# Row steps of 32x32 inverses moved to GpSimd, with other margins in a hand-written list schedule

## The chip, the cores and the metric

One core of a Trainium2 chip. The metric is the device time of one execution in microseconds; lower is better.

## The reference

One layer of a hybrid trunk on x of 512 x 1024 in float32: a mixer of four branches (Mamba-2, a gated linear recurrence, retention, RWKV-7) on one combined input projection, gated, merged and projected, then a convolutional feed-forward block, with root-mean-square norms between. The change touches the RWKV-7 branch, which for each of 16 heads of 64 runs this over 512 steps:

```python
def step(state, inp):
    r_t, w_t, k_t, v_t, kk_t, b_t = inp
    sk = jnp.einsum('bhvk,bhk->bhv', state, kk_t)
    state = (state * w_t[:, :, None, :] - sk[..., None] * b_t[:, :, None, :]
             + v_t[..., None] * k_t[:, :, None, :])
    return state, jnp.einsum('bhvk,bhk->bhv', state, r_t)
```

The kernel does it in chunks of 64 steps, so that each chunk needs the inverse of a unit triangular 64x64 matrix, which is put together from inverses of 32x32 blocks.

## The kernel before, in words

**Weights.** A weight block of 128 x 1024 is loaded by SP into `raw` (4 buffers, L452). `split` (L446) casts it on ACT to a high part `whi` (L447, 3 buffers) and takes the low part `wlo` on DVE (L448, 3 buffers). A product is three matmuls for each of 8 slices (L466 to L468): 24 matmuls of 128 x 512 a block, into one of three PSUM buffers `acc`. These are the long work of PE; all four branches, the gates, the output projection and the feed-forward block (from L1289) are made of them.

**RWKV in pairs of heads.** Eight pairs j run one behind the other. `rwkv_a1(j)` makes the projections and decays. `rwkv_a2(j)` builds the scaled operands (L701 on GpSimd, L702 to L705 on DVE), the products of a chunk with itself (L719), and the block matrices `ab`. These go to DRAM (`nd`, L764) and come back as `nt` (L767), one 32x32 matrix of 32 to a partition, its columns dealt out over four groups of partitions. Then 31 row steps follow (L769 to L775): each multiplies a column of `nt` with a row of `xr` into `prod` and adds that to the later rows of `xr`; (31 - jj) rows of jj//4 + 1 columns in step jj. Both instructions are on DVE. `xr` and a transposed copy (L777) go to DRAM as `xd` and `xtd` (L781, L782) and come back as `x11`, which has the buffer of `xr` (L787, shown as xr in the profile), and `tt` (L790). `rwkv_b(j)` joins the blocks with 32x32 matmuls (L801, L811) and runs the chunks in turn: L824, L826, L828, L829, L830, L832, L835. L869 makes the output, L870 sends it to DRAM for the branch product. Most tiles of a pair have one buffer, so pair j+1 reaches L719 when pair j is through its chunks.

**What fills PE meanwhile.** Generators give the other three branches and, once these are through, the branch products with their gates (L1217 to L1249) to fill PE. The last branch product (L1286) needs the RWKV output.

**The planner.** At the end `_order` (L390) takes all instructions of the program, plays them through a model of the five queues (`_run`, L236), improves the priorities in `_RUNS` rounds, keeps the best plan and ties each engine's instructions into that order; on the chip each engine follows it and waits where an operand is late. Costs stand in `_cost` (L114): for a GpSimd operation

```python
return 250.0 + n * (0.9 if kind == "InstMemset" else 1.0 if kind == "InstTensorCopy" else 2.4), _HOP
```

with n elements per partition and 60 ns for the way to another engine. On PE a "short" product (one that doesn't go to `acc`) comes ahead of weight products, but only if its operands have been ready for `_MARGIN` ns (L309); 32-row matmuls are `small`, those that follow each other in one tile stay together, and a change to or from them is charged 500 ns. A DMA is charged 450 ns of its queue, its bytes on a common wire at 330 bytes a ns, and 1500 ns until it has landed (L337, L338). A DVE operation of several operands that starts while GpSimd is busy is charged up to 0.7 of its time more (L327).

Of the kernel before, what the change touches and what calls it, by code (L numbers as in the profile page):

```python
# [15 lines left out]
P = 128  # L16
# [29 lines left out]
for _key in ([("lora", 0), ("lora", 1)]  # L46
# [16 lines left out]

_TABLES = {"Exp": ("exp",), "Tanh": ("exp", "sigmoid", "gelu", "silu"), "Sigmoid": ("sigmoid",), "Sqrt": ("sqrt",),
           "Gelu_apprx_tanh": ("gelu",), "Silu": ("silu",)}
_MARGIN = 50.0
_RUNS = 12
_HOP = 60.0
_SWITCH = 500.0


def _base(name):
# [74 lines left out]
def _graph(nc):  # L147


    import types  # L150
    E = mybir.EngineType
    ins = list(nc.cur_bb.bb.instructions)
    N = len(ins)
    preds = [set() for _ in range(N)]
    news, tiles_of = [[] for _ in range(N)], [[] for _ in range(N)]
    hist, users, tag_of, pool_of, queue, bufs = {}, {}, {}, {}, {}, {}
    released, gate, psum = [], {}, set()
    real, last_new, opener, after = [], {}, {}, [set() for _ in range(N)]
    small = [isinstance(i, mybir.InstMatmult) and i.ins[0].bass_ap.shape[0] <= 32 for i in ins]
    for k, i in enumerate(ins):  # L160
        if "Boundary" in type(i).__name__:
            text = i.concise()
            pool = text.split("pool=")[1].split()[0]
            if "op=release" in text:
                released.append(pool)
            else:
                gate[pool] = list(released)
            continue
        real.append(k)
        for write, args in ((False, i.ins), (True, i.outs)):  # L170
            for a in args:
                ap = getattr(a, "bass_ap", None)
                if ap is None or not hasattr(ap.tensor, "slot_key"):
                    continue
                t = ap.tensor
                name = t.name
                p0, p1, m = _region(ap)
                bank = t.space == bass.MemoryType.PSUM
                if name not in hist:
                    tag = str(t.slot_key())  # L180
                    hist[name], tag_of[name], users[name] = [], tag, []
                    if tag in last_new and last_new[tag] != k:
                        after[k].add(last_new[tag])
                    last_new[tag] = k
                    queue.setdefault(tag, []).append(name)
                    bufs[tag] = t.tag_meta.bufs or 1
                    pool_of[name] = tag.rstrip("')").split("_")[-2]
                    if bank:
                        psum.add(pool_of[name])
                    news[k].append(name)  # L190
                lst = hist[name]
                if opener.setdefault(name, k) != k:
                    after[k].add(opener[name])
                for o, w, q0, q1, b in lst:
                    if (write or w or bank) and o != k and q0 < p1 and p0 < q1 and b & m:
                        preds[k].add(o)
                if write or bank:
                    lst[:] = [x for x in lst if x[0] == k or not (p0 <= x[2] and x[3] <= p1 and x[4] & ~m == 0)]
                lst.append((k, write, p0, p1, m))
                if name not in tiles_of[k]:  # L200
                    tiles_of[k].insert(0 if write else len(tiles_of[k]), name)
                    users[name].append(k)
    for k in real:
        after[k] -= preds[k]
        preds[k] |= after[k]

    lead, last = {}, None
    for k in real:
        if ins[k].engine == E.PE:
            if not small[k]:  # L210
                last = None
            elif last is not None and tiles_of[last][0] == tiles_of[k][0]:
                lead[k] = last = lead[last]
            else:
                lead[k] = last = k
    for k, l in lead.items():
        preds[l] |= {o for o in preds[k] if lead.get(o) != l}
        after[l] |= {o for o in after[k] if lead.get(o) != l}
        if k != l:
            preds[k].add(l)  # L220
            after[k].add(l)
    succ = [[] for _ in range(N)]
    for k in real:
        for o in preds[k]:
            succ[o].append(k)
    gates = {}
    for p, old in gate.items():
        gates[p] = [q for q in old if (q in psum) == (p in psum)]
    acc = [i.engine == E.PE and _base(i.outs[0].bass_ap.tensor.name) == "acc" for i in ins]
    cost = [None] * N  # L230
    for k in real:
        cost[k] = _cost(ins[k])
    return types.SimpleNamespace(**locals())


def _run(g, prio, margin):  # L236
# [8 lines left out]
    engines = [E.PE, E.DVE, E.Activation, E.Pool, E.SP]  # L245
    free = {e: 0.0 for e in engines}
    pend, ready, order = {e: [] for e in engines}, {e: [] for e in engines}, {e: [] for e in engines}
    held, table, wire, was = [], "", 0.0, False
    queue = {t: list(q) for t, q in g.queue.items()}
    room = {t: [(0.0, "")] * b for t, b in g.bufs.items()}  # L250
    n_users = {t: len(u) for t, u in g.users.items()}
# [5 lines left out]
    def offer(k):  # L257
# [6 lines left out]
        for n in g.news[k]:  # L264
# [4 lines left out]
                behind.setdefault(k, []).append(old)  # L269
            for q in g.gates.get(g.pool_of[n], ()):  # L270
                est[k] = max(est[k], pool_end.get(q, 0.0))
        heapq.heappush(pend[ins[k].engine], (est[k], k))
        return True

    def try_held():
# [16 lines left out]
    while len(seq) < len(real):  # L292
        best = None
        for e in engines:
            if ready[e]:
                t = free[e]
            elif pend[e]:
                t = max(free[e], pend[e][0][0])
            else:
                continue  # L300
            if best is None or t < best[0]:
                best = (t, e)
        t, e = best
        while pend[e] and pend[e][0][0] <= t:
            k = heapq.heappop(pend[e])[1]
            heapq.heappush(ready[e], (-1.0 if g.lead.get(k, k) != k else prio[k], k))
        early = []
        if e == E.PE:
            while ready[e] and not g.acc[ready[e][0][1]] and ready[e][0][0] >= 0 and est[ready[e][0][1]] + margin > t:  # L309
                early.append(heapq.heappop(ready[e]))  # L310
            if early and not ready[e]:
                heapq.heapify(early)
                ready[e], early = early, []
        k = heapq.heappop(ready[e])[1]
        for x in early:
            heapq.heappush(ready[e], x)
        i = ins[k]
        dur, tail = g.cost[k]
        if e == E.Activation and type(i).__name__ == "InstActivation":
            sets = _TABLES.get(str(i.func).split(".")[-1])  # L320
            if sets and table not in sets:
                table = sets[0]
                dur += 1283.0
        if e == E.PE and g.small[k] != was:
            was = g.small[k]
            dur += _SWITCH
        if e == E.DVE and free[E.Pool] > t and len(i.ins) > 1 and not g.tiles_of[k][-1].startswith(("ra", "rb", "acc")):  # L327
            dur *= 1.0 + 0.7 * min(1.0, (free[E.Pool] - t) / dur)
        order[e].append(k)
# [4 lines left out]
        if type(i).__name__ == "InstDMACopy":  # L334
            free[e] = t + (450.0 if e == E.SP else 100.0)
            dur_of[k] = free[e] - t
            wire = max(wire, t + 450.0) + 4.0 * i.outs[0].bass_ap.size() / 330.0  # L337
            done[k] = wire + 1500.0  # L338
        opened = bool(g.news[k])
        for s in g.succ[k]:  # L340
            left[s] -= 1
            est[s] = max(est[s], t if k in g.after[s] else t + dur if ins[s].engine == e and e != E.SP else done[k])
            if not left[s]:
                if g.news[s]:
                    held.append(s)
# [16 lines left out]
def _latest(g, r, chained):  # L362
# [11 lines left out]
            for u in g.users[m]:  # L374
                need.setdefault(u, []).append(k)
    for k in reversed(r.seq):
        e = g.ins[k].engine
        whole = r.done[k] - r.start[k]
        v = r.end - whole
        if k in nxt:  # L380
            v = min(v, late[nxt[k]] - r.dur[k])
        for s in g.succ[k]:
            v = min(v, late[s] - (0.0 if k in g.after[s] else r.dur[k] if g.ins[s].engine == e and e != E.SP else whole))
        for s in need.get(k, ()):
            v = min(v, late[s] - whole)
        late[k] = v
# [3 lines left out]
def _order(tc, nc):  # L390
# [7 lines left out]
    for n in range(_RUNS):  # L398
# [1 line left out]
        if best is None or r.end < best.end:  # L400
            best = r
        late = _latest(g, r, [PE])
        prio = [first[k] if g.ins[k].engine == PE else late[k] for k in range(g.N)]
    behind = mybir.DependencyInfo(mybir.DependencyClass.NoSync, mybir.DependencyReason.DATA)
    for seq in best.order.values():
        for a, b in zip(seq, seq[1:]):
# [4 lines left out]
def tile_hybrid_block(ctx, tc, x, wts, wzdt, lora, lruw, cpack, consts, rettab, nfin, out):  # L411
# [37 lines left out]

    def wraw(kind, j):  # L450
        n = 1088 if kind == "zdt" else 1024
        raw = wp.tile([P, 1088], F32, name="raw", bufs=4)  # L452
        nc.sync.dma_start(out=raw[:, 0:n], in_=wzdt[j] if kind == "zdt" else wts[_BLK[(kind, j)]])
        return raw, n

    def wsplit(raw, n):
        hi = wp.tile([P, 1088], F32R, name="whi", bufs=3)
        lo = wp.tile([P, 1088], F32R, name="wlo", bufs=3)
        split(hi[:, 0:n], lo[:, 0:n], raw[:, 0:n])
        return hi, lo  # L460
# [232 lines left out]
    def rwkv_a2(j, prep):  # L693
# [76 lines left out]
        for jj in range(31):  # L770
            n, m = 31 - jj, jj // 4 + 1
            pr = rkb.tile([P, 32, 8], F32, name="prod", bufs=1)
            nc.vector.tensor_tensor(out=pr[:, 0:n, 0:m], in0=nt[:, jj, jj + 1:32].unsqueeze(2).broadcast_to([P, n, m]),
                                    in1=xr[:, jj:jj + 1, 0:m].broadcast_to([P, n, m]), op=ALU.mult)
            nc.vector.tensor_tensor(out=xr[:, jj + 1:32, 0:m], in0=xr[:, jj + 1:32, 0:m], in1=pr[:, 0:n, 0:m], op=ALU.add)  # L775
        xt = rkb.tile([P, 8, 32], F32, name="prod", bufs=1)
        nc.vector.tensor_copy(out=xt, in_=xr.rearrange("p i c -> p c i"))  # L777
        xd = dr.tile([16, 32, 32], F32, name="xd", bufs=2)
# [750 lines left out]
```

## Time and profile before

| what | value |
|---|---|
| median of 3 runs | 1600.75 us (1598.83 to 1601.36) |
| the profiled execution, device time | 1597.41 us |
| its span, first to last instruction | 1595.6 us |
| mean granted clock of TensorE | 0.981 |

PE is the matrix engine, PEld its weight loads, DVE the vector engine, ACT the scalar engine, POOL is GpSimd, SP the queue that issues nearly all DMAs. A name such as `raw<-in_wts_dram` tells the tile written and what is read. Each wait is put down to what ended it.

### The profile page before, as it was taken

The numbers are of one execution on the slowest core, as the hardware profiler recorded it, in microseconds if no ns is written. First come the engines' busy times: TensorE is split into PE (matmuls) and PEld (weight loads), VectorE is DVE, ScalarE is ACT, GpSimd is POOL, SyncE is SP. The second block draws the span as 40 slices with busy tenths as digits, with TensorE's granted clock in tenths as the row PEclk, the third lists the DMA queues.
The fourth block names the chain that finished last, engine by engine and source line by source line (L and its number), as shares of the span: only waits on it lengthen the run. The fifth ranks groups of instructions, "written<-read, shape, count | busy, mean of one in ns | idle before, by whom it ended". The sixth has DMA issues, their size and how long they took to land.

```text
span 1595.6 us, 22214 instructions
## 1 busy us (share of the span) xinstructions
PE 1546.5 (97%) x8324; PEld 1297.7 (81%) x8324; DVE 1085.2 (68%) x2334; ACT 733.9 (46%) x1198; POOL 60.7 (4%) x78
## 2 busy tenths in 40 slices
PE   7999989999999999999999999999999999999998
PEld 6878868887788888977878878888888888888886
DVE  6797888887888897887765966435335666566233
ACT  6653476447754585358422622323224544444123
POOL 0100000000001000001000100000000000000000
PEclk9999999999999998998999999999999999999999
DMA  5243233233143233353442432434232322323321
GB/s 207 81 126 85 79 109 106 80 106 97 54 144 105 69 104 101 97 163 112 153 128 67 148 102 74 149 103 132 95 130 95 106 92 95 104 92 109 102 94 53
DMA packets 108461, 169.46 MB, mean 106 GB/s; under 512 B 54833, under 2 KB 64305, under 8 KB 108353
## 3 DMA queue, kind: packets, MB, share of 16 engines
q1 hardware_dynamic: 107632, 166.92, 33.0%
q8 instruction: 66, 1.08, 0.3%
q10 hardware_dynamic: 720, 1.11, 0.2%
q14 instruction: 43, 0.34, 0.1%
HBM read 150.66 MB, written 15.24 MB: 104 GB/s over the span
## 4 chain that ended last, share of the span: by engine, by line
PE 85%; DVE 7%; DMA 3%; SPq 2%; ACT 1%; issue 1%; DVEq 0%; ACTq 0%
PE acc L467 19%; PE acc L466 19%; PE acc L468 19%; PE acc L1302 3%; PE acc L1303 3%; PE acc L1301 3%; PE rb L824 2%; PE acc L587 1%; PE ra L719 1%; PE acc L588 1%; PE acc L589 1%; PE rb L828 1%; SPq L782 1%; DVE wlo L448 1%; PE inn L443 1%
## 5 line engine op out<-in xcount | busy, mean ns | idle before, releaser
L466 PE MATMUL acc<-hh,whi 128*128 128x512 f32 (+1 forms) x1240 | 496.7, 401 | 6.3 <-DVE pr L611 4.3
L467 PE MATMUL acc<-hh,wlo 128*128 128x512 f32 (+1 forms) x1240 | 495.7, 400 | 0.5 <-DVE wlo L448 0.4
L468 PE MATMUL acc<-hl,whi 128*128 128x512 f32 (+1 forms) x1240 | 493.4, 398 | 0.1
L448 DVE TENSOR_TENSOR wlo<-raw,whi 128x1024 fp32r<-128x1024 f32 x228 | 278.7, 1224 | 206.5 <-ACT whi L447 205.4
L447 ACT CAST whi<-raw 128x1024 fp32r<-128x1024 f32 x228 | 239.1, 1049 | 390.0 <-PE acc L468 210.0
L466 PEld LDWEIGHTS acc<-hh,whi 128*128 128x128 f32 x1240 | 236.5, 191 | 51.3 <-DVE pr L611 5.2
L467 PEld LDWEIGHTS acc<-hh,wlo 128*128 128x128 f32 x1240 | 236.5, 191 | 43.7 <-issue 1.9
L468 PEld LDWEIGHTS acc<-hl,whi 128*128 128x128 f32 x1240 | 236.3, 191 | 42.6 <-issue 1.2
L468 PE MATMUL acc<-yl,whi 128*128 128x512 f32 x256 | 102.6, 401 | 0.0
L466 PE MATMUL acc<-yh,whi 128*128 128x512 f32 x256 | 102.5, 401 | 0.0
L467 PE MATMUL acc<-yh,wlo 128*128 128x512 f32 x256 | 102.2, 399 | 0.0
L587 PE MATMUL acc<-whi,hh 128*128 128x256 f32 (+1 forms) x256 | 78.1, 307 | 0.7 <-DVE sm L906 0.7
L588 PE MATMUL acc<-wlo,hh 128*128 128x256 f32 (+1 forms) x256 | 77.9, 305 | 0.0
L589 PE MATMUL acc<-whi,hl 128*128 128x256 f32 (+1 forms) x256 | 76.9, 301 | 0.0
L1301 PE MATMUL acc<-whi,gh 128*128 128x512 f32 x176 | 69.4, 395 | 0.0
L1303 PE MATMUL acc<-whi,gl 128*128 128x512 f32 x176 | 69.4, 395 | 0.0
L1302 PE MATMUL acc<-wlo,gh 128*128 128x512 f32 x176 | 69.4, 395 | 0.0
L1356 DVE SCALAR_TENSOR_TENSOR fc<-acc,fw,fc 128x511 f32<-128x511 f32 x88 | 65.7, 747 | 4.0 <-ACT fc L1354 2.5
L775 DVE TENSOR_TENSOR xr<-xr,prod 128x60 f32<-128x60 f32 (+24 forms) x248 | 56.9, 229 | 8.1
L468 PEld LDWEIGHTS acc<-yl,whi 128*128 128x128 f32 x256 | 48.6, 190 | 9.6 <-DVE yl L448 0.2
L466 PEld LDWEIGHTS acc<-yh,whi 128*128 128x128 f32 x256 | 48.6, 190 | 9.2
L906 DVE SCALAR_TENSOR_TENSOR sm<-acc,cp,sm 128x511 f32<-128x511 f32 (+2 forms) x72 | 53.6, 745 | 3.6 <-ACT sm L904 2.3
(334 smaller groups left out, 2454.8 us busy)
## 6 DMA issues: line engine op xcount, KB each, us to landing
raw<-in_wts_dram SPq DMA_DIRECT2D x226, 512.0 KB, 3.3
yr<-y SPq DMA_DIRECT2D x32, 256.0 KB, 3.5
y<-sm SPq DMA_DIRECT2D x24, 256.0 KB, 2.2
nt<-nd SPq DMA_DIRECT2D x32, 128.0 KB, 2.7
sm<-acd SPq DMA_DIRECT2D x16, 256.0 KB, 4.1
x<-in_x_dram SPq DMA_DIRECT2D x4, 512.0 KB, 6.2
sm<-sm SPq DMA_DIRECT2D x32, 64.0 KB, 2.0
ym<-bg SPq DMA_DIRECT2D x16, 128.0 KB, 1.8
```

What stands on the lines that cost most here:

```text
L447: nc.scalar.copy(out=hi, in_=src)
L448: nc.vector.tensor_tensor(out=lo, in0=src, in1=hi.bitcast(F32), op=ALU.subtract)
L466: nc.tensor.matmul(ps, wh, xh, start=first, stop=False)
L467: nc.tensor.matmul(ps, wl, xh, start=False, stop=False)
L468: nc.tensor.matmul(ps, wh, xl, start=False, stop=last)
L587: nc.tensor.matmul(o, hh[:, ko, t], wh[:, s], start=ko == 0, stop=False)
L588: nc.tensor.matmul(o, hh[:, ko, t], wl[:, s], start=False, stop=False)
L589: nc.tensor.matmul(o, hl[:, ko, t], wh[:, s], start=False, stop=ko == KT - 1)
L1301: nc.tensor.matmul(ps[i], xh[:, ko, t], w[0][:, s], start=ko == 0, stop=False)
L1302: nc.tensor.matmul(ps[i], xh[:, ko, t], w[1][:, s], start=False, stop=False)
L1303: nc.tensor.matmul(ps[i], xl[:, ko, t], w[0][:, s], start=False, stop=ko == 2 * nblk - 1)
L1356: nc.vector.scalar_tensor_tensor(out=t[:, s:], in0=ps[:, :S - s], scalar=fw[:, o + 2 - s:o + 3 - s], in1=t[:, s:], op0=ALU.mult, op1=ALU.add)
```

## The change

Both instructions of each of the 31 row steps go from DVE to GpSimd (62 for a pair of heads, 496 in all). `whi` has four buffers instead of three, `raw` three instead of four. In the planner: the margin of a short product is 100 ns instead of 50, and 300 ns where it is a 32-row matmul; a read into SBUF from the scratch tensors xd, xtd, y, ym or acd is charged 2500 ns instead of 1500 until it has landed; the first weight product after a short one is charged 17 ns more; eight rounds instead of twelve. Weight products and short ones have lists of their own (the choice between them follows the same rule as before).

```diff
-_MARGIN = 50.0
-_RUNS = 12
+_MARGIN = 100.0
+_RUNS = 8
 _HOP = 60.0
 _SWITCH = 500.0
+_BACK = 17.0
...
-        early = []
         if e == E.PE:
-            while ready[e] and not g.acc[ready[e][0][1]] and ready[e][0][0] >= 0 and est[ready[e][0][1]] + margin > t:
-                early.append(heapq.heappop(ready[e]))
-            if early and not ready[e]:
-                heapq.heapify(early)
-                ready[e], early = early, []
-        k = heapq.heappop(ready[e])[1]
-        for x in early:
-            heapq.heappush(ready[e], x)
+            while ready[e]:
+                k = heapq.heappop(ready[e])[1]
+                heapq.heappush(weights if g.acc[k] else shorts, (-1.0 if g.lead.get(k, k) != k else prio[k], k))
+            early = []
+            while shorts and shorts[0][0] >= 0 and est[shorts[0][1]] + (300.0 if g.small[shorts[0][1]] else margin) > t:
+                early.append(heapq.heappop(shorts))
+            if weights and not shorts:
+                k = heapq.heappop(weights)[1]
+            else:
+                if not shorts:
+                    shorts, early = early, []
+                    heapq.heapify(shorts)
+                k = heapq.heappop(shorts)[1]
+            for x in early:
+                heapq.heappush(shorts, x)
+        else:
+            k = heapq.heappop(ready[e])[1]
...
+            if not run and g.acc[k]:
+                dur += _BACK
+            run = run + 1 if g.acc[k] else 0
...
-            done[k] = wire + 1500.0
+            done[k] = wire + (2500.0 if i.outs[0].bass_ap.tensor.space != bass.MemoryType.DRAM and
+                              _base(i.ins[0].bass_ap.tensor.name) in ("xd", "xtd", "y", "ym", "acd") else 1500.0)
...
-        raw = wp.tile([P, 1088], F32, name="raw", bufs=4)
+        raw = wp.tile([P, 1088], F32, name="raw", bufs=3)
...
-        hi = wp.tile([P, 1088], F32R, name="whi", bufs=3)
+        hi = wp.tile([P, 1088], F32R, name="whi", bufs=4)
...
             pr = rkb.tile([P, 32, 8], F32, name="prod", bufs=1)
-            nc.vector.tensor_tensor(out=pr[:, 0:n, 0:m], in0=nt[:, jj, jj + 1:32].unsqueeze(2).broadcast_to([P, n, m]),
+            nc.gpsimd.tensor_tensor(out=pr[:, 0:n, 0:m], in0=nt[:, jj, jj + 1:32].unsqueeze(2).broadcast_to([P, n, m]),
                                     in1=xr[:, jj:jj + 1, 0:m].broadcast_to([P, n, m]), op=ALU.mult)
-            nc.vector.tensor_tensor(out=xr[:, jj + 1:32, 0:m], in0=xr[:, jj + 1:32, 0:m], in1=pr[:, 0:n, 0:m], op=ALU.add)
+            nc.gpsimd.tensor_tensor(out=xr[:, jj + 1:32, 0:m], in0=xr[:, jj + 1:32, 0:m], in1=pr[:, 0:n, 0:m], op=ALU.add)
```

## Rows read from the trace of the kernel before

**Rows 1.** The page: span, and busy time of each engine.

```profile
span 1595.6 us, 22214 instructions
...
PE 1546.5 (97%) x8324; PEld 1297.7 (81%) x8324; DVE 1085.2 (68%) x2334; ACT 733.9 (46%) x1198; POOL 60.7 (4%) x78
```

**Rows 2.** Busy time of each engine by stretch of 40 us, granted clock, DMA share.

```profile
120.00:160.00 40.00, 38.88 (x298) 35.28 (x298) 31.92 (x83) 13.05 (x25) 2.91 (x2) 0.91 0.33 85
480.00:520.00 40.00, 38.68 (x313) 35.40 (x312) 32.25 (x75) 16.44 (x42) 4.16 (x3) 0.96 0.37 105
600.00:640.00 40.00, 36.63 (x287) 33.54 (x286) 30.21 (x66) 23.16 (x46) 2.95 (x2) 0.87 0.32 88
720.00:760.00 40.00, 37.25 (x233) 30.55 (x232) 28.44 (x56) 31.59 (x48) 5.82 (x3) 0.83 0.40 119
800.00:840.00 40.00, 37.46 (x224) 30.49 (x222) 26.73 (x81) 12.21 (x20) 1.23 (x2) 0.97 0.42 119
840.00:880.00 40.00, 39.96 (x205) 33.59 (x205) 21.54 (x58) 9.64 (x19) 1.90 (x2) 0.95 0.22 71
1040.00:1080.00 40.00, 40.00 (x178) 33.11 (x177) 13.74 (x15) 9.34 (x11) 0.00 (x0) 1.00 0.27 93
```

**Rows 3.** PE's waits, longest in total first: total us, times, longest us.

```profile
PE inn L443 <- DVE nxn L504: 10.1, 1, 10.1
...
PE rb L801 <- DMA xr<-xd: 9.4, 10, 2.5
...
PE acc L466 <- DVE pr L611: 4.3, 1, 4.3
...
PE rb L811 <- DMA tt<-xtd: 3.1, 2, 2.6
...
PE rb L443 <- DVE ab L859: 1.9, 3, 1.5
...
PE acc L467 <- DVE wlo L448: 0.4, 1, 0.4
```

**Rows 4.** PE's timeline at the fifth and sixth hand-over: start, duration, instruction, idle before.

```profile
605.70 1.45 PE L801 MATMUL rb<-xr,ab 32*32 32x32 f32 x32 [0.68 <-DMA xr<-xd]
...
611.19 1.33 PE L811 MATMUL rb<-tt,xr 32*32 32x32 f32 x32 [2.59 <-DMA tt<-xtd]
...
724.71 0.39 PE L467 MATMUL acc<-hh,wlo 128*128 128x512 f32 x1
...
727.81 0.28 PE L801 MATMUL rb<-xr,ab 32*32 32x32 f32 x2 [2.48 <-DMA xr<-xd]
728.35 1.12 PE L801 MATMUL rb<-xr,ab 32*32 32x32 f32 x30 [0.27 <-DMA xr<-xd]
...
730.00 0.63 PE L467 MATMUL acc<-hh,wlo 128*128 128x512 f32 x1
```

**Rows 5.** The row steps on DVE: groups, the first and seventh pair, DVE's busy time.

```profile
L775 DVE TENSOR_TENSOR xr<-xr,prod 128x60 f32<-128x60 f32 (+24 forms) x248 | 56.9, 229 | 8.1
L773 DVE TENSOR_TENSOR prod<-nt,xr 128x60 f32<-128x60 f32 (+24 forms) x248 | 52.3, 211 | 4.6 <-DMA nt<-nd 2.3
...
L775 DVE TENSOR_TENSOR xr<-xr,prod x31: 168/224/586, 93.4 to 130.5; 128x60 f32<-128x60 f32 x3, 128x28 f32<-128x28 f32 x2, 128x54 f32<-128x54 f32 x2, 128x48 f32<-128x48 f32 x2
L775 DVE TENSOR_TENSOR xr<-xr,prod x31: 166/221/241, 807.2 to 827.6; 128x60 f32<-128x60 f32 x3, 128x28 f32<-128x28 f32 x2, 128x54 f32<-128x54 f32 x2, 128x48 f32<-128x48 f32 x2
...
L775 DVE TENSOR_TENSOR xr<-xr,prod 128x60 f32<-128x60 f32 (+24 forms) x31 | 7.4, 239 | 1.0
L773 DVE TENSOR_TENSOR prod<-nt,xr 128x60 f32<-128x60 f32 (+24 forms) x31 | 6.5, 211 | 0.1
...
93.00:131.00 38.00, 38.00 (x196) 32.17 (x195) 33.68 (x105) 21.32 (x38) 1.22 (x2) 1.00 0.36 117
```

**Rows 6.** GpSimd's operations, from the lines' own views and GpSimd's groups.

```profile
L820 POOL MEMSET sv<- x16: 144/147/148, 72.7 to 900.1; 64x64 f32 x16
L959 POOL MEMSET bg<- x8: 518/520/521, 73.0 to 595.0; 64x512 f32 x8
L701 POOL TENSOR_TENSOR bk<-pk,di x16: 1274/1642/2246, 69.7 to 898.2; 64x512 f32<-64x512 f32 x16
L701 POOL TENSOR_TENSOR bk<-pk,di 64x512 f32<-64x512 f32 x16 | 26.0, 1626 | 290.9 <-issue 144.0 <-ACT di L689 108.0 <-DVE sm L906 38.4
```

**Rows 7.** Timelines of GpSimd and DVE from 69.6 us.

```profile
69.65 3.02 POOL L701 TENSOR_TENSOR bk<-pk,di 64x512 f32<-64x512 f32 x2 [65.19 <-ACT di L689]
...
69.75 1.75 DVE L704 SCALAR_TENSOR_TENSOR bk<-pa,di 64x512 f32<-64x512 f32 x1
...
73.84 0.69 DVE L704 SCALAR_TENSOR_TENSOR bk<-pa,di 64x512 f32<-64x512 f32 x1
```

**Rows 8.** The RWKV output, and the branch products' evictions: ns, first and last start.

```profile
L869 DVE TENSOR_TENSOR yu<-yu,rb x8: 678/685/690, 214.5 to 995.2; 128x512 f32<-128x512 f32 x8
...
L1246 DVE TENSOR_TENSOR gt<-acc,gt x24: 684/692/692, 916.0 to 1174.7; 128x512 f32<-128x512 f32 x24
```

**Rows 9.** DMA issues with KB and us to landing; waits for the weights' buffers.

```profile
tt<-xtd SPq DMA_DIRECT2D x32, 32.0 KB, 3.0
xr<-xd SPq DMA_DIRECT2D x16, 32.0 KB, 2.0
...
ACT whi L447 <- PE acc L468: 210.0, 75, 5.6
SPq L453 <- DVE wlo L448: 674.1, 145, 15.6
```

More of the change, by code (lines that the diff above doesn't have):

```diff
@@ L228, in _graph @@
         gates[p] = [q for q in old if (q in psum) == (p in psum)]
+    eng = [getattr(i, "engine", None) for i in ins]
     acc = [i.engine == E.PE and _base(i.outs[0].bass_ap.tensor.name) == "acc" for i in ins]
@@ L247, in _run @@
     pend, ready, order = {e: [] for e in engines}, {e: [] for e in engines}, {e: [] for e in engines}
-    held, table, wire, was = [], "", 0.0, False
+    held, table, wire, was, run = [], "", 0.0, False, 1
+    weights, shorts = [], []
     queue = {t: list(q) for t, q in g.queue.items()}
@@ L271, in offer @@
                 est[k] = max(est[k], pool_end.get(q, 0.0))
-        heapq.heappush(pend[ins[k].engine], (est[k], k))
+        heapq.heappush(pend[g.eng[k]], (est[k], k))
         return True
@@ L294, in _run @@
         for e in engines:
-            if ready[e]:
+            if ready[e] or (e == E.PE and (weights or shorts)):
                 t = free[e]
@@ L323, in _run @@
                 dur += 1283.0
-        if e == E.PE and g.small[k] != was:
-            was = g.small[k]
-            dur += _SWITCH
+        if e == E.PE:
+            if g.small[k] != was:
+                was = g.small[k]
+                dur += _SWITCH
+            if not run and g.acc[k]:
+                dur += _BACK
+            run = run + 1 if g.acc[k] else 0
         if e == E.DVE and free[E.Pool] > t and len(i.ins) > 1 and not g.tiles_of[k][-1].startswith(("ra", "rb", "acc")):
@@ L341, in _run @@
             left[s] -= 1
-            est[s] = max(est[s], t if k in g.after[s] else t + dur if ins[s].engine == e and e != E.SP else done[k])
+            est[s] = max(est[s], t if k in g.after[s] else t + dur if g.eng[s] == e and e != E.SP else done[k])
             if not left[s]:
@@ L376, in _latest @@
     for k in reversed(r.seq):
-        e = g.ins[k].engine
+        e = g.eng[k]
         whole = r.done[k] - r.start[k]
@@ L382, in _latest @@
         for s in g.succ[k]:
-            v = min(v, late[s] - (0.0 if k in g.after[s] else r.dur[k] if g.ins[s].engine == e and e != E.SP else whole))
+            v = min(v, late[s] - (0.0 if k in g.after[s] else r.dur[k] if g.eng[s] == e and e != E.SP else whole))
         for s in need.get(k, ()):
@@ L402, in _order @@
         late = _latest(g, r, [PE])
-        prio = [first[k] if g.ins[k].engine == PE else late[k] for k in range(g.N)]
+        prio = [first[k] if g.eng[k] == PE else late[k] for k in range(g.N)]
     behind = mybir.DependencyInfo(mybir.DependencyClass.NoSync, mybir.DependencyReason.DATA)
```

## The prediction

> **What bounds the kernel now.** First the page's busy times: PE works 1546.5 of 1595.6 us [rows 1], so 49 us of idle time are all that scheduling could win, plus what PE loses at a low clock. The first 10.1 of them are the wait for the first normalised rows [rows 3], the rest lies in the middle and at the end. Next the table by stage [rows 2]: the stretch 1040 to 1080 is pure weight work, 178 matmuls in 40 us, 0.225 us each, clock 1.00, PE full. Of the stretches that hold the hand-overs spoken of below, six have a granted clock of 0.83 to 0.97. The clock has two levels, 2.4 and 1.2 GHz; a stretch of 40 us at mean c spent 2 x (1 - c) x 40 us at the lower one and lost half of that. The six lose 3.6 + 1.6 + 5.2 + 6.8 + 1.2 + 2.0 = 20.4 us. Then PE's waits [rows 3]: the longest group in the middle is L801 waiting for xr read back from xd (9.4 us, 10 times), and L811 for tt read back from xtd (3.1 us, twice): 12.5 us, at the hand-over from the 32x32 inverses to the chunk recurrence. Last the timeline there [rows 4]: in the fifth pair of heads PE stands still 0.68 and 2.59 us, in the sixth 2.48 and 0.27 us, and behind the latter L467 takes 0.63 us where it took 0.39: the clock fell. Idle PE at the hand-over and the low clock behind it belong together: the stretches of the two longest waits are the two with the lowest clock.
>
> So the bound is PE, in an order written out beforehand by a planner; the losses are places where the real chain came later than planned. That order is static, so a planner that is wrong by some microseconds in a chain is paid for in each of the eight pairs.
>
> **The inverses.** 62 steps a pair, 496 in all, leave DVE: 52.3 + 56.9 = 109.2 us [rows 5], 13.65 us a pair. They took longer by the clock, since other DVE work stood between them: 93.4 to 130.5 us in the first pair, 807.2 to 827.6 in the seventh, 37 and 20 us.
>
> On GpSimd no such step was run, so its price has bounds. The steps write the sum over jj of (31 - jj)(jj//4 + 1) = 1560 elements per partition, twice: 3120 for a pair, 50 a step. The planner charges 250 ns + 2.4 ns an element (L139): 62 x 0.25 + 3120 x 0.0024 = 23.0 us. From the rows [rows 6]: memsets of 64 and 512 elements take 0.147 and 0.520 us, so 0.094 us fixed; the undisturbed two-input step of 512 takes 1.274 us, so 2.30 ns an element above that: 62 x 0.094 + 3120 x 0.0023 = 13.0 us. If the fixed part of a two-input step is the planner's 0.25, the element is 2.0 ns and the pair 21.7 us. I take the middle, 17 us: the steps are as small as the memset but of the other kind. Now the disturbance. The two-input step has a mean of 1.626 against 1.274 us [rows 6], and next to it DVE's L704 takes 1.75 where it takes 0.69 alone [rows 7]: each waited for the other. The stretch, 1.28, gives 17 x 1.28 = 21.8 us, just under the planned 23.0. Upper end: in the first inverse's 38 us DVE is busy 33.7, 13.9 of it the steps themselves [rows 5]; were all the other 19.8 (52%) closed to GpSimd, 17 / 0.48 = 35 us. I take 21.8, by the only GpSimd row of this kind in company.
>
> The Trainium skill (GPSIMD Engine Reference, section 3.1) gives 4497 ns for a two-input step of 2048 elements; an estimate from that and the row's 1274 ns is 2.10 ns an element and 0.20 us fixed, 18.9 us a pair. With the same stretch that is 24.2 us, 1.2 above the plan, and the sum below would come out near 1591 instead of 1582. No run here shows that size.
>
> **On or off the path.** Where the plan holds, the inverse's length costs nothing: weight work covers it. The last pair's output is made at 995 us [rows 8]; the last branch product, which needs it, evicts its eight blocks 11.2 us apart up to 1175, so begins near 1085. So 90 us of branch work stand in reserve, 11 us a pair. DVE's 109 us are worth little by themselves: PE's waits for DVE or ACT in the middle come in groups of under 2 us, and one of 4.3 (L466 for pr) [rows 3]. I take 3 us, between nothing and 10.
>
> **The hand-over.** Reads of xd, xtd (and y, ym, acd) are planned to land 2.5 instead of 1.5 us after the wire, and a small matmul waits 300 instead of 50 ns after its operands. So L801 and L811 are placed 1.25 us later, with weight matmuls ahead of them. Where the profile has xr<-xd landing in 2.0 and tt<-xtd in 3.0 us [rows 9], the extra microsecond covers most of the spread, not the worst. The fifth and sixth hand-over keep 3.27 - 1.25 and 2.75 - 1.25; the other waits, 6.5 us in five hand-overs, mostly vanish. Gain: 2 x 1.25 + 4.8 = 7 us (0 to 12.5). The low clock shrinks with the waits, by about half: 20.4 x 0.45 = 9 us (0 to 20).
>
> **Waits added.** The copy L777 stays on DVE and now waits for GpSimd; behind it in DVE's queue stand wlo subtractions and evictions. SP's L781 waits for xr, with weight loads behind it. Both are hidden while the plan is kept: a block of 24 matmuls lasts 5.4 us, two finished blocks are ahead, and PE waited for wlo 0.4 us in all [rows 3]. If GpSimd is late that cover goes, block by block.
>
> **The rest.** whi 3 to 4, raw 4 to 3: nothing. ACT waited 210 us for a free whi, SP 674 us for a free raw [rows 9], while PE hardly waited for weights; the cover gone would cost up to one block, 5.4 us, once or twice. Margin 100 for all short products, 17 ns charged per return, eight plans instead of twelve: another order of the same matmuls; -3 to +3 us, taken as nothing.
>
> Sum: -7 - 9 - 3 = -19 us on the profiled span of 1595.6: 1576.6, with the 1.8 us around it 1578.4. That execution was 3.3 us under the median, so 1582 us against 1600.75.
>
> **Rivals.** *GpSimd late against its plan* (slower). What speaks for it: rows 7, and that DVE is busy 89% of the first inverse's time. Then L777 blocks DVE, L781 blocks SP and PE stands at L801, eight times. At 27 us instead of 23.0 (17 us of steps, ports closed 37% of the time) the waits are 8 x 4 = 32 for 12.5, and the clock falls every time, 8 x 4.8 = 38 us for 20 (between the fifth's 5.2 and the mean of the six, 3.4): +19.5 + 18 - 3 = +34, 1635 us. It decides from about 25 us a pair: 8 x 2 = 16 us take the gain away. Against it: a blocked DVE leaves the ports to GpSimd, which bounds the lateness.
> The Trainium skill (SBUF — State Buffer, section "SBUF: two separate sides") says that the port pair that DVE and GpSimd share is an exclusive lock for a whole instruction. Rows 7 agree: 1.75 us instead of 0.69.
>
> *Moved, not removed* (same): the chain through GpSimd and back comes 1.25 us later than planned, the longer transfers are eaten up, and waits and clock stay as they were: 1601 us.
>
> *The hand-over wholly clean* (more gain): all 12.5, all 20.4 and 10 us of other waits: 1558 us.
>
> **Chances.** Forecast 0.46, clean hand-over 0.08, same 0.13, late GpSimd 0.33. So faster 0.54, same 0.13, slower 0.33, where 0.2% is 3.2 us, about what a measurement of this kernel can tell from no change. The forecast's own range is 1570 to 1594. The whole range, 1560 to 1640, leaves out the clean end and a GpSimd of more than 27.5 us.
>
> **What would show it.** Right: 62 GpSimd steps from first to last in 18 to 23 us a pair; waits of L801 and L811 together at 6 us or less; stretches below clock 0.9 gone or one; DVE's busy time near 980 us (its delayed operations longer by a few us). Wrong: steps of 0.4 us and more spacing, DVE's L777 and SP's L781 waiting for POOL, PE's wait at L801 of several us each time with the clock at half behind it. A rise of waits for wlo would show the lost raw buffer.

## The result and the profile after

The changed kernel takes 1617.84 us (median of 4 runs) where the kernel before, run beside it, takes 1599.79: a ratio of 1.0115, 95% interval 1.0092 to 1.0137, 18 us slower. The forecast was 1582 us and the wrong way; the rival that ended slower, GpSimd late against its plan, is what happened. The lines of the kernel stand 16 further down than before (L775 is L791, L777 is L793, L781 is L797, L801 is L817, L811 is L827, L1145 is L1161).

The page: span, and busy time of each engine, as [rows 1].

```profile
span 1613.9 us, 22216 instructions
...
PE 1546.2 (96%) x8324; PEld 1294.5 (80%) x8324; DVE 1005.3 (62%) x1838; ACT 725.2 (45%) x1191; POOL 257.7 (16%) x574
```

PE works as long as before; its idle time went from 49.1 to 67.7 us, by 18.6, which is the whole loss of the span (18.3). DVE lost 80 us of its busy time, not 109. Little of the difference is GpSimd's doing: added up by groups, DVE's operations take 1149 us before and 1048 after, so those that stayed grew by some 9 us. The largest group, the subtractions of the weight split, before and after:

```profile
L448 DVE TENSOR_TENSOR wlo<-raw,whi 128x1024 fp32r<-128x1024 f32 x228 | 278.7, 1224 | 206.5 <-ACT whi L447 205.4
L464 DVE TENSOR_TENSOR wlo<-raw,whi 128x1024 fp32r<-128x1024 f32 x228 | 282.9, 1242 | 283.8 <-PE acc L483 175.6
```

The rest is a way of counting: records of operations that follow each other overlap (in a timeline below, the copy at 124.38 lasts 0.39 us and the next operation begins at 124.68), and the page counts such time once. So the 109 us, a sum of single durations, are more than what leaves the page's busy time with the steps.

The mean granted clock is 0.975 after 0.981: 40.3 us of full clock are missing instead of 30.3. PE's busy time did not grow by these 10 us. A part of the low clock falls into PE's waits, where it costs nothing: in the first pair's wait, below, the clock falls 2.4 us before PE goes on. What became of the rest no row shows.

PE's waits, as [rows 3]: total, times, longest.

```profile
PE rb L817 <- DMA xr<-xd: 16.1, 4, 6.7
PE inn L1161 <- DVE sm L1147: 12.7, 2, 6.9
...
PE inn L1034 <- DVE sm L1029: 3.6, 1, 3.6
PE ra L676 <- ACT kk L673: 3.5, 1, 3.5
...
PE rb L827 <- DMA tt<-xtd: 0.9, 2, 0.6
```

The hand-over, 12.5 us before, is now 17.0 us, and a wait for a DVE operation of the Mamba branch, 0.6 us before, has grown to 12.7 us. The waits of DVE and of SP's queue show why:

```profile
DVE prod L793 <- POOL xr L791: 47.1, 8, 8.3
...
SPq L797 <- POOL xr L791: 53.1, 7, 10.0
```

In each of the eight pairs DVE stands at the transposing copy, 5.9 us on the average, because GpSimd's last step has not come; SP stands at the store behind the same steps. The first pair, in the timelines of GpSimd, DVE and PE (start and duration in us, instruction, idle time before it and what ended it):

```profile
90.08 0.51 POOL L789 TENSOR_TENSOR prod<-nt,xr 128x31 f32<-128x31 f32 x1 [17.42 <-DMA nt<-nd]
...
91.05 0.26 POOL L789 TENSOR_TENSOR prod<-nt,xr 128x30 f32<-128x30 f32 x1
91.39 0.30 POOL L791 TENSOR_TENSOR xr<-xr,prod 128x30 f32<-128x30 f32 x1
91.76 1.26 POOL L789 TENSOR_TENSOR prod<-nt,xr 128x29 f32<-128x29 f32 x1
...
94.19 0.28 POOL L789 TENSOR_TENSOR prod<-nt,xr 128x54 f32<-128x54 f32 x1
94.54 0.33 POOL L791 TENSOR_TENSOR xr<-xr,prod 128x54 f32<-128x54 f32 x1
94.95 0.27 POOL L789 TENSOR_TENSOR prod<-nt,xr 128x52 f32<-128x52 f32 x1
...
116.15 0.29 POOL L789 TENSOR_TENSOR prod<-nt,xr 128x60 f32<-128x60 f32 x1
...
123.86 0.20 POOL L789 TENSOR_TENSOR prod<-nt,xr 128x8 f32<-128x8 f32 x1
124.14 0.20 POOL L791 TENSOR_TENSOR xr<-xr,prod 128x8 f32<-128x8 f32 x1
```

```profile
91.69 1.22 DVE L464 TENSOR_TENSOR wlo<-raw,whi 128x1024 fp32r<-128x1024 f32 x1 [0.62 <-ACT lh L463]
...
124.38 0.39 DVE L793 COPY prod<-xr 128x256 f32<-128x256 f32 x1 [8.30 <-POOL xr L791]
124.68 0.68 DVE L1147 TENSOR_TENSOR sm<-sm 128x512 f32<-128x512 f32 x1
```

```profile
118.14 0.39 PE L483 MATMUL acc<-hh,wlo 128*128 128x512 f32 x1
125.42 0.69 PE L1161 MATMUL inn<-bg,sm 128*128 128x64 f32 x2 [6.89 <-DVE sm L1147]
...
126.44 0.63 PE L482 MATMUL acc<-hh,whi 128*128 128x512 f32 x1
```

Three stretches there, columns as in [rows 2]: the whole of the pair's steps, and the two parts of PE's wait.

```profile
90.08:124.34 34.26, 28.45 (x139) 23.34 (x137) 21.30 (x36) 18.85 (x33) 29.51 (x66) 0.98 0.38 127
118.60:123.00 4.40, 0.00 (x0) 0.00 (x0) 0.00 (x0) 1.09 (x2) 3.38 (x14) 1.00 0.00 0
123.00:125.40 2.40, 0.00 (x0) 0.00 (x0) 1.02 (x3) 0.00 (x0) 1.03 (x5) 0.50 0.00 0
```

And GpSimd alone, while DVE stands at the copy:

```profile
116.15:124.34 8.19, 6.39 (x24) 0.92 0.10 35
```

Read together: two undisturbed steps of 54 elements begin 0.35 and 0.41 us before the next one, although each is only 0.28 and 0.33 us long. 0.38 us is exactly what the planner charges (250 + 2.4 x 54 ns). At 116 DVE reaches the copy and stands; from then on 24 steps take 8.19 us, 0.34 each, where the plan charges 8.35. Only 6.39 us of them are steps: 0.08 us lie between the end of one and the start of the next. So the plan has the undisturbed price, and no reserve for company: the step that meets a wlo subtraction at 91.69 takes 1.26 us instead of 0.26, until DVE's operation is over. The pair's steps take from 90.1 to 124.3 us, 34.3 us, where the plan has 23.0; over the eight pairs (28.1 to 35.0) the mean is 31.3. Not all of that is steps: 66 operations stand in the stretch above, 62 of them steps. The order puts other GpSimd operations between them, mostly these copies, two to a pair, and memsets:

```profile
L762 POOL COPY uv<-sv x16: 602/610/1633, 105.4 to 935.9; 64x512 f32<-64x512 f32 x16
```

From start to start they take 2.1 us of a pair; the steps alone take 29.2 us, 6.2 more than charged. Behind the copy L793 stands L1147, PE waits 6.89 us for it, and the first weight matmuls after that take 0.63 us: the granted clock is 0.50, its lower level.

The Trainium skill (SBUF — State Buffer, section "SBUF: two separate sides") calls the port pair that the two engines share an exclusive lock held for a whole instruction. The 1.26 us beside 0.26 agrees. The Trainium skill also says (Perfetto Trace Analysis, section "GPSIMD Engine Instruction") to time GpSimd by the spacing of starts and not by reported durations. The 0.28 us beside a spacing of 0.35 agrees, and this is where the forecast went wrong, below.

Table by stage, three stretches of the changed kernel, columns as in [rows 2]:

```profile
120.00:160.00 40.00, 33.88 (x281) 30.89 (x282) 29.80 (x63) 12.41 (x32) 5.92 (x16) 0.91 0.33 85
...
440.00:480.00 40.00, 31.84 (x187) 27.61 (x185) 22.40 (x28) 16.05 (x29) 26.30 (x58) 0.89 0.46 126
...
960.00:1000.00 40.00, 35.38 (x221) 28.99 (x220) 15.45 (x37) 7.95 (x17) 0.00 (x0) 0.87 0.29 76
```

PE stands still 4.6 to 8.2 us in each, and the clock is down in the same stretches. The last one has no GpSimd operation: PE stands at L817 there, 4.5 us, at the last pair's hand-over.

### The profile page after: what moved, and what is told of

The parts are those of the page before. It is cut to its first block, busy times and chain, and to the rows that moved or that the text cites. A ratio compares the mean times of both kernels' runs of the same rounds, so it can differ in the third digit from the quotient of the medians.

```text
span 1613.9 us, 22216 instructions
## 1 busy us (share of the span) xinstructions
PE 1546.2 (96%) x8324; PEld 1294.5 (80%) x8324; DVE 1005.3 (62%) x1838; ACT 725.2 (45%) x1191; POOL 257.7 (16%) x574
## 4 chain that ended last, share of the span: by engine, by line
PE 47%; POOL 3%; DMA 2%; DVE 1%; SPq 1%; issue 1%; ACT 0%; POOLq 0%; DVEq 0%; ACTq 0%
PE acc L484 11%; PE acc L482 11%; PE acc L483 11%; PE acc L1318 3%; PE acc L1319 3%; PE acc L1317 3%; POOL xr L791 2%; POOL prod L789 1%; DMA yr<-y 1%; PE rb L840 1%; DMA nt<-nd 0%; PE rb L844 0%; PE ra L735 0%; DMA nd<-ab 0%; PE rb L848 0%
## 5 line engine op out<-in xcount | busy, mean ns | idle before, releaser
L464 DVE TENSOR_TENSOR wlo<-raw,whi 128x1024 fp32r<-128x1024 f32 x228 | 282.9, 1242 | 283.8 <-PE acc L483 175.6
L789 POOL TENSOR_TENSOR prod<-nt,xr 128x60 f32<-128x60 f32 (+24 forms) x248 | 98.5, 397 | 221.5 <-DMA nt<-nd 141.8
L791 POOL TENSOR_TENSOR xr<-xr,prod 128x60 f32<-128x60 f32 (+24 forms) x248 | 98.9, 399 | 19.4
L1370 ACT ACTIVATE fc<-acc,fw 128x512 f32<-128x512 f32 x44 | 34.3, 780 | 93.2 <-PE acc L484 93.2
L717 POOL TENSOR_TENSOR bk<-pk,di 64x512 f32<-64x512 f32 x16 | 24.8, 1548 | 259.8 <-ACT di L705 259.2
```

Of the source, the lines that this page charges most:

```text
L464: nc.vector.tensor_tensor(out=lo, in0=src, in1=hi.bitcast(F32), op=ALU.subtract)
L789: nc.gpsimd.tensor_tensor(out=pr[:, 0:n, 0:m], in0=nt[:, jj, jj + 1:32].unsqueeze(2).broadcast_to([P, n, m]), in1=xr[:, jj:jj + 1, 0:m].br ...
L791: nc.gpsimd.tensor_tensor(out=xr[:, jj + 1:32, 0:m], in0=xr[:, jj + 1:32, 0:m], in1=pr[:, 0:n, 0:m], op=ALU.add)
```

## The experiments

Theory A: GpSimd's steps take longer than the plan says, some 6 us a pair in the changed kernel (the expectations reckon with 8.3, which holds the other GpSimd operations too); the static order then makes DVE, SP and PE wait for them, eight times. Theory B: the new settings and buffers made a worse order, and the move is harmless. Theory C: the move costs time through the ports, whatever the plan says. All times are medians; the kernel before took 1599 to 1600.5 us beside each set.

**1. The steps back on DVE, all else as changed.**

```diff
-            nc.gpsimd.tensor_tensor(out=pr[:, 0:n, 0:m], ...
+            nc.vector.tensor_tensor(out=pr[:, 0:n, 0:m], ...
-            nc.gpsimd.tensor_tensor(out=xr[:, jj + 1:32, 0:m], ...
+            nc.vector.tensor_tensor(out=xr[:, jj + 1:32, 0:m], ...
```

> The changed kernel with its row steps back on DVE; margins, transfers and buffers stay changed. Theory A (GpSimd's steps come later than planned, 31.3 us a pair by the trace against 23.0 charged, and DVE, SP and PE stand behind them): 1580 to 1600 us, PE's waits at L817 under 6 us in all where the changed kernel has 16. Theory B (the planner's new settings and the buffers make the worse order, the move does no harm): 1610 us or more. Theory C (the steps on GpSimd cost the time through the shared ports, whatever the plan says): as A.

1573.3 us, ratio to before 0.9826 (0.981 to 0.9842). This fits A or C, and B falls: settings and buffers gain 27 us with the steps on DVE, and the move costs the changed kernel 44.5. The waits at L817 are 1.9 us; those at L827 are 7.1.

```profile
PE rb L827 <- DMA tt<-xtd: 7.1, 7, 2.9
...
PE rb L817 <- DMA xr<-xd: 1.9, 3, 1.4
```

**2. The move kept, its price in the plan put right.** In the planner's cost, for two-input GpSimd operations of under 100 elements:

```diff
     if i.engine == E.Pool:
+        if kind == "InstTensorTensor" and n < 100:
+            return 340.0 + n * 3.27, _HOP
```

> The changed kernel, with a row step on GpSimd charged 340 ns + 3.27 ns an element in the plan: 31.3 us a pair, what the trace showed, instead of 23.0. A: DVE's wait at the copy behind the steps falls from 47 us to under 15, PE's waits for xr<-xd and for DVE fall with it, 1575 to 1602 us. B: 1610 to 1625 us. C: the waits fall, but the time stays at 1605 to 1620 us.

1575.3 us, ratio 0.9837 (0.9821 to 0.9854). The same instructions on the same engines, 42.6 us faster than the changed kernel, by one price in the planner. A holds and C falls. The 31.3 us were read with the other GpSimd operations in them; the steps alone take 31.8 us in this kernel, so the charge fits. DVE's wait at the copy (L795 here):

```profile
DVE prod L795 <- POOL xr L793: 3.9, 2, 3.2
```

**3. More prices.** The same edit with 285 + 2.7 n (26.1 us a pair) and with 425 + 4.1 n (39.1 us).

> The changed kernel with a row step on GpSimd charged 285 ns + 2.7 ns an element, 26.1 us a pair (23.0 gave 1617.8 us, 31.3 gave 1575.3). A (time lost in proportion to what the plan leaves out): 5 of the 8.3 missing us a pair are still missing, so 1595 to 1607 us, DVE's wait at the copy 20 to 40 us. Rival (any other order of the matmuls would have done as well, the price only shuffled it): 1570 to 1580, or 1612 and more.

> The changed kernel with a row step on GpSimd charged 425 ns + 4.1 ns an element, 39.1 us a pair, 8 us more than it takes. A: branch work covers the longer planned chain, PE has no waits at the hand-over, 1568 to 1580 us. Rival (a longer chain is paid for at the end of the recurrence or in order): 1585 us or more.

1601.9 us (ratio 1.0007, 0.9992 to 1.0021) and 1569.1 us (0.98, 0.9773 to 0.9828). With the two others:

| charged for a pair, us | DVE's wait at the copy, us | time, us |
|---|---|---|
| 23.0 (the change) | 47.1 | 1617.8 |
| 26.1 | 37.0 | 1601.9 |
| 31.3 | 3.9 | 1575.3 |
| 39.1 | none | 1569.1 |

Each microsecond that the plan leaves out costs about 5 us of the whole (16 for 3.1, then 26.6 for 5.2); a charge that is too high costs nothing here. Four points in a row speak against a price that merely shuffles the order. What they do not part: the planner charges more for a DVE operation that starts while GpSimd is busy, so a longer charge for the steps gives DVE's operations more time too. How much of the gain comes by that way no run shows. With 39.1 us charged the pairs take 28.1 to 43.0 us, mean 33.8 (the steps alone 31.7), DVE never stands at the copy, and the page and PE's waits read:

```profile
span 1566.3 us, 22231 instructions
...
PE 1530.3 (98%) x8324; PEld 1284.5 (82%) x8324; DVE 1004.2 (64%) x1838; ACT 736.9 (47%) x1200; POOL 272.6 (17%) x574
```

```profile
PE rb L829 <- DMA tt<-xtd: 2.8, 5, 1.2
...
PE rb L819 <- DMA xr<-xd: 1.4, 2, 0.8
```

Of the 47.6 us between the two profiled spans, 31.7 are PE's idle time (36.0 instead of 67.7). The other 16 are its busy time, for the same 8324 matmuls: the mean granted clock is 0.991 instead of 0.975. This version beats both kernels.

**4. Nothing of DVE waits for the steps.** The changed kernel with its copy on GpSimd too.

```diff
-        nc.vector.tensor_copy(out=xt, in_=xr.rearrange("p i c -> p c i"))
+        nc.gpsimd.tensor_copy(out=xt, in_=xr.rearrange("p i c -> p c i"))
```

> The changed kernel with the transposing copy L793 on GpSimd too, so that nothing of DVE's queue waits for the end of the steps; the steps are charged too little as before. A: DVE's 47 us of waiting there go and PE's 12.7 us at L1161 with them, while the waits at L817 stay (12 us or more): 1598 to 1610 us. B and C: 1613 to 1623 us.

1635.1 us, ratio 1.021 (1.019 to 1.0229): slower than the changed kernel, where A expected 1598 to 1610 us. The expectation was wrong in its direction. The waits still fit A's cause, but that reading was made after the run:

```profile
PE rb L817 <- DMA xr<-xd: 65.3, 9, 12.7
```

With DVE free to go on, it stays in GpSimd's way to the end: it is busy 65% of the time from a pair's first step to its last, 55% in the changed kernel. The pairs take 29.8 to 39.2 us, mean 33.6, and the lateness reaches PE at one place, 8.2 us a pair. Without the other GpSimd operations (2.0 us) the steps take 31.6 us, 8.6 more than the plan charges: about what PE waits. So DVE's standing still at the copy cost time and bounded GpSimd's lateness at once: it let GpSimd run undisturbed.

**5. The move alone, in the kernel before.**

> The kernel before with nothing but the 62 row steps of a pair moved to GpSimd: old margins, transfers and buffers. A: slower than the changed kernel, 1620 to 1650 us, since the plan has 1.25 us less in reserve at each hand-over; PE waits at L801 over 25 us in all. B: 1595 to 1606 us. C: 1612 to 1622 us.

1622.4 us, ratio 1.0143 (1.0122 to 1.0164); 47.1 us of DVE's wait at the copy, as in the changed kernel, and 25.5 us of PE at L801. As A expected. The new settings and buffers, worth 27 us with the steps on DVE, are worth 4.6 with this lateness: 1.25 us of reserve does little where 6 are missing (the steps alone take 29.5 us here).

**6. The move alone, with 425 + 4.1 n charged.**

> The kernel before with only its steps on GpSimd (1622.4 us) and a step charged 425 ns + 4.1 ns an element. If the wrong charge alone makes the move cost time, the kernel is back at the level before or a little under, and doesn't need the other settings for that: 1588 to 1603 us. If the move costs by itself in the old settings: 1608 us or more.

1577.1 us, ratio 0.9862 (0.9841 to 0.9884): 45 us better than 5 and better than expected. So the wrong charge is the whole cost of the move, in the old settings as in the new. Why it comes 22.6 us below the kernel before is not settled. It is not the hand-over, where PE waits 13.4 us in all, 12.5 in the kernel before:

```profile
PE rb L803 <- DMA xr<-xd: 11.0, 8, 5.8
...
PE rb L813 <- DMA tt<-xtd: 2.4, 2, 2.1
```

PE's busy time is 17 us less (1529.6, mean clock 0.990). DVE is 78 us freer, and the order is another one; nothing here parts the two.

**7. What the settings do with the steps on DVE.** Six kernels: the planner's settings without the buffers; longer transfers alone; margins alone; the 17 ns alone; transfers and margins together; transfers and the 17 ns together. The buffers alone make a seventh. Each has the lines of the change for its part and none of the others; eight rounds instead of twelve are in the first alone.

> The changed kernel with its row steps on DVE and the buffers as before (raw 4, whi 3): the planner's new settings alone. With the buffers too it was 1573.3 us. If the settings carry the gain: 1572 to 1582 us. If settings and buffers only gain together: 1588 us or more.

> The kernel before, steps on DVE, with the 2500 ns for reads from the scratch tensors as its only change. If the transfers carry the 27 us that the planner's settings and buffers gained with the steps on DVE: 1575 to 1588 us, with the 12.5 us of waits at L801 and L811 down to 6 or less. If margins, the 17 ns or the buffers carry them: 1592 us or more.

> The kernel before, steps on DVE, with the margins of short products (100 ns, 300 ns for 32-row matmuls) as its only change. If the margins carry the larger part of the gain, fewer waits of under 1 us and less time at the low clock: 1578 to 1588 us. If not: 1592 us or more.

> The kernel before, steps on DVE, with the 17 ns charged for a return to weight products as its only change (some 710 returns, 12 us of PE time that the plan left out, which makes PE later than planned against the chain). If the plan's truth about PE matters as that about GpSimd does: 1585 to 1593 us. If it is nothing, as forecast: 1595 to 1603 us.

> The kernel before, steps on DVE, with the longer transfers and the new margins together. Alone they gave 1593.1 and 1598.5 us; all planner settings together 1580.2. If these two carry the gain together (the hand-over as forecast: 16 us less): 1577 to 1586 us, waits at L801 and L811 under 5 us. If the 17 ns for a return are needed with them: 1588 to 1596 us.

> The kernel before, steps on DVE, with the longer transfers and the 17 ns for a return together. Alone they gave 1593.1 and 1608.2 us. If the return's cost turns to a gain once the hand-over is late enough: 1577 to 1588 us. If it costs whatever goes with it: 1597 us or more.

> The kernel before with whi in four buffers and raw in three as its only change. If the buffers are worth nothing, as forecast: 1595 to 1605 us. If they carry the 27 us: 1580 us or less.

| with the steps on DVE | time, us | ratio to before, 95% interval |
|---|---|---|
| planner's settings, buffers as before | 1580.2 | 0.9897 (0.9873 to 0.992) |
| longer transfers | 1593.1 | 0.9954 (0.9936 to 0.9973) |
| margins | 1598.5 | 0.9991 (0.9971 to 1.0011) |
| 17 ns for a return | 1608.2 | 1.0061 (1.0033 to 1.0089) |
| transfers and margins | 1586.4 | 0.9916 (0.9897 to 0.9935) |
| transfers and 17 ns | 1592.4 | 0.996 (0.9944 to 0.9975) |
| buffers | 1595.4 | 0.9971 (0.9954 to 0.9988) |

The settings gain together, not one by one: the margins give nothing alone and some 7 us on top of the transfers; the 17 ns cost 9 us alone and nothing with the transfers. Three results missed their expectations: the 17 ns alone lie above both ranges, with the transfers they lie between the two, and transfers and margins lie 0.4 us past theirs. Each setting also gives another order of thousands of instructions, so some microseconds of a single number may be luck. The sum, 19 us, is shown; how it divides among the settings is not. Nor is it the waits at the hand-over that decide: the margins alone took these from 12.5 to 4.6 us and gained nothing.

```profile
PE rb L801 <- DMA xr<-xd: 3.2, 7, 0.7
...
PE rb L811 <- DMA tt<-xtd: 1.4, 4, 0.7
```

**8. Still later transfers.** The kernel with 39.1 us charged, and 3500 instead of 2500 ns for the reads from the scratch tensors.

> The changed kernel with a row step charged 425 ns + 4.1 ns an element (1569.1 us) and the reads from the scratch tensors 3500 instead of 2500 ns. If waits at the hand-over are what is left: 1562 to 1568 us. If the order is settled by other things: 1567 to 1575 us.

1573.2 us, ratio 0.9847 (0.9828 to 0.9866): no better than 1569.1. With 1.4 and 2.8 us of waits left at the hand-over there was little more to win there.

## Why the prediction was wrong

**The step that failed** is the price of a row step on GpSimd: "I take the middle, 17 us", and the stretch of 1.28 that made it 21.8, "just under the planned 23.0". Both factors were too small, and a third part was left out. Undisturbed, the steps take what the plan says (8.19 us for 24 of them, 8.35 planned), so 23 us a pair: 0.37 us a step of 50 elements, where the forecast's 17 us are 0.27. The forecast took durations of single operations [rows 6] for the pace of a chain of them. Between two steps lie 0.08 us, 5 us in 62 steps, most of what was missing. The stretch is 31.6 / 23.0 = 1.37 with DVE going on beside it (experiment 4), not 1.28: the 1.28 came from long steps [rows 6], while a short one can meet a much longer DVE operation, as the 1.26 us instead of 0.26 show. That this is the reason for the larger stretch is argued, not tested. Last, other GpSimd operations stand between the steps, 2.0 us a pair, which the forecast did not count. Together 33.6 us instead of 21.8. The bound of 35 us that the prediction set aside was the right neighbourhood.

What followed from the wrong price is shown by experiments 2, 3 and 6: with the steps' charge raised and nothing else changed, the loss is gone.

**The rival was right in kind.** It named L777, SP's L781 and L801, and these are the places. Its price was off in both directions: it had 27 us a pair where the pairs take 31 to 34, and 1635 us where the changed kernel took 1618. That experiment 4 took just 1635 us is chance: PE waits 65 us at the hand-over there, where the rival had 32. It undervalued its own counterargument, that a DVE that stands still leaves the ports free. Its threshold, "from about 25 us a pair", 2 us over the plan, was too early: in experiment 3 the kernel is level with the one before where some 5 us of the steps' 31.2 are still left out, since the new settings' and buffers' own gain of 27 us has to be eaten up first.

**The hand-over's gain came out near the forecast in its sum, not in its terms**, and only without the move. Forecast were 7 us of waits and 9 of low clock; the planner's settings with the steps on DVE gave 19. Their waits for xd and xtd fell from 12.5 to 3.2 us, but other waits came in their place: PE's idle time went from 49.1 to 48.2 us only.

```profile
span 1578.2 us, 22220 instructions
...
PE 1530.0 (97%) x8324; PEld 1285.0 (81%) x8324; DVE 1085.5 (69%) x2334; ACT 740.4 (47%) x1203; POOL 60.5 (4%) x78
```

Nearly all of the gain is PE's busy time, 16.5 us less at a mean granted clock of 0.993. So the term of the clock was too small, the term of the waits too large, and that the sum fits is luck. Why the clock stays up with as much idle time is open. With the move none of it showed, for the waits grew past the reserve.

**DVE's relief** was taken as 3 us. DVE's busy time is 1005 us, not "near 980": 109 us of summed durations were only 80 of its busy time. With the steps charged high enough the move gives 1569.1 us, with the steps on DVE the same settings give 1573.3; the intervals of the two ratios overlap, so in the new settings no worth of the relief is shown. **Buffers** were costed at nothing; alone they gave 4.6 us, just clear of no change, and on top of the planner's settings 7 us (1580.2 to 1573.3, whose intervals do not meet).

**The chances.** A third for the late GpSimd was too little. What spoke for it stood in the prediction: a price never measured, within 6% of the plan's, multiplied by eight, in a static order. The forecast needed that price to come out below the plan's, and still gave 0.54 to faster.

## What to carry to other kernels

In a kernel whose order is fixed beforehand, a step moved to another engine needs its price in company put into the plan first; a charge that is too high cost nothing here, one that was 6 to 9 us a pair too low cost 42 us in eight rounds. Time a chain of small operations by the spacing of their starts, not by the length of one; count what else the engine does in between, and look at what the other engine does meanwhile. Look first at who stands in the queue behind the instruction that must now wait for the other engine: here the copy, and behind it L1147, for which PE waited 12.7 us. What an engine gains by losing work is read from its busy time, not from the sum of the durations.

## What was not expected of the hardware

A two-input GpSimd step of 8 elements takes 0.20 us and its successor starts 0.28 us after it, one of 54 elements 0.28 to 0.33 and 0.35 to 0.41 us. An estimate from these is 2.2 ns an element, so that some 0.26 us of a step do not depend on its size. A chain of them beside a DVE that is busy 65% of the time runs 1.37 times as long as planned (31.6 us, 23.0 planned), and at the planned pace as soon as DVE stands still. PE's busy time for the same 8324 matmuls went from 1546 to 1530 us with the price put right, at a granted clock of 0.991 instead of 0.975; with the planner's settings alone it came as low while PE's idle time hardly changed.
